# Compact score tables with one masked copy, and GpSimd's sums and products moved to VectorE

## The chip, the cores and the metric

The kernel runs on one core of a Trainium2 chip. A core has five engines that work side by side, each with its own instruction queue: TensorE (PE in the profile) does matrix products and transposes into PSUM; VectorE (DVE), ScalarE (ACT) and GpSimd (POOL) do elementwise work; SyncE (SP) issues most DMAs. PEld is TensorE's loading of weights, which overlaps its products. An engine takes its instructions in order, and an instruction waits until the data that it needs are there. The metric is the time of one execution on the device, in microseconds (us); lower is better.

## What is computed

One layer of an encoder: half a step of a SwiGLU feed-forward network (FFN), a mixer, another half FFN step and a last norm, over 1024 tokens of width 1024, in fp32. The mixer has two groups of heads that share one input projection: attention with four query and two key/value heads, and a gated recurrence with four heads that runs in both directions. In the reference, cut to what matters here:

```python
def hgrn2_chunk_scan(q, k, v, log_f):          # per head; f = exp(log_f), k = 1 - f
    ...
    scores = jnp.einsum('nhtd,nhtsd,nhsd->nhts', qc, decay, kc)
    intra = jnp.einsum('nhts,nhse->nhte', scores, vc)
    ...

def hgrn2_bidirectional(q, zf_fwd, zf_bwd, i, g, lb, out_gain):
    ...
    o_dir = hgrn2_chunk_scan(q_dir, k_dir, v_dir, g_dir)
    o = o_dir[:bsz] + flip(o_dir[bsz:])
    o = rms_norm(o, out_gain).reshape(bsz, seq_len, REC_WIDTH)
    return o * jax.nn.silu(g)

def gqa_bidirectional(q, k, v, q_gain, k_gain):
    q = apply_axial_rope(rms_norm(q, q_gain), tables) * (HEAD_DIM ** -0.5)
    k = apply_axial_rope(rms_norm(k, k_gain), tables)
    ...

def hybrid_mixer(x, ...):
    ...
    return jnp.concatenate([attn, rec.astype(attn.dtype)], axis=-1) @ w_out
```

`out_gain` is one weight for each of the 128 channels of a head, the same for all four heads.

## The kernel before

The stages follow one another: FFN 1, the mixer's input stage (`mixer_in`, with the recurrence in `hgrn`), attention with the output projection (`attention`), FFN 2. All products have fp32 operands split into a rounded high part and a rest (`split`, L89: a ScalarE copy, then a VectorE subtraction), with three products for one.

**The recurrence.** `hgrn(n, ...)` (L892) works on one head: 128 channels on the partitions, 1024 tokens in eight chunks of 128 along the columns. The scores within a chunk are built from the diagonal and seven levels with blocks of 1, 2, 4 ... 64 tokens. The diagonal's key is the sum `kd` of the keys of both directions (L915, GpSimd). At each level TensorE makes a table of local scores of key blocks with queries (`block_product`, L880: two products of 64 by 64 per chunk); the table is right only where the two tokens lie in sibling blocks, so VectorE copies it under a 0/1 mask (`copy_predicated`, L961) into the head's matrix `A`. For the levels below 64 only the two diagonal 64 by 64 quarters of a chunk are used, so each level takes two masked copies, of partitions 0 to 63 and 64 to 127. Level 64 fills the two other quarters, with two ScalarE copies (L958). Between the levels VectorE multiplies keys and queries by the decay of the sibling block (L948, L952), ScalarE copies what stays (L939), and VectorE multiplies pairs of decays (`tot`, L971 and L974). Then come transposes of the keys (`ktp`, L982), their ScalarE copies (L984), products with the values (`U`, L992), a scan over chunks on VectorE (L1000) and the output `o` (L1014).

**The norm.** `head_norm` (L1021) squares on ScalarE, sums on VectorE (L1030), takes the root on GpSimd (`rstd`, L86), multiplies on VectorE (L1033, L1038) and multiplies by the gain on GpSimd (L1043). It serves the recurrence's output (`on`), stored to DRAM by an SP DMA, and the rotary parts.

**Rotary parts.** `roped` (L1055) takes the query projection `aq` (1024 columns) and the key projection `ak` (512 columns) in four parts each: `head_norm`, a swap of halves by ScalarE copies (L1071), the cosine product on VectorE (L1076), the sine product on GpSimd (L1077), their sum on VectorE (L1078), an SP DMA.

**The order.** The heads of the recurrence run one after another with high priority; TensorE's other projections are fitted between: `ri` (values) and head 1's projections beside head 0, `aq` and head 2's beside head 1, head 3's beside head 2, `rgk` (recurrence gates and attention keys, which are roped) beside head 3, then `rgv`. Wide PSUM tiles of these projections (`pp`) and of the recurrence (`ph`) have two buffers each. The order on every queue is made when the program is built, by a scheduler that goes by its own estimates of durations, so it is made anew for changed code.

**Attention.** For each of eight row blocks `rec_out` (L1267) multiplies the stored recurrence output by its gate on GpSimd, transposes it into `rT`, splits that into `recT` (L1275) and projects it. `vectors` (L764) loads the small weights and the masks, in the middle of FFN 1.

Of the kernel before, what the change touches and what calls it, by code (L numbers as in the profile page):

```python
# [13 lines left out]
F32 = mybir.dt.float32  # L14
F32R = mybir.dt.float32r
I32 = mybir.dt.int32
U8 = mybir.dt.uint8
# [27 lines left out]
class Trunk:  # L45
    def __init__(self, ctx, tc, io):
# [6 lines left out]
        pool("base", bufs=1).tile([P, 248], F32, name="base")  # L53
# [710 lines left out]
    def vectors(self, tmp):  # L764
# [3 lines left out]
        rows = tmp.tile([n_lb + NQ, P], F32, name="rows", tag="raw")  # L768
        nc.sync.dma_start(rows[:n_lb, :], io["rec_lb_logits"].rearrange("s j (h p) -> (s j h) p", p=P))
        nc.sync.dma_start(rows[n_lb:, :], io["attn_out_norm"].rearrange("(h p) -> h p", p=P))  # L770
        pt = self.ps("rows_T", "u")
        n = n_lb + NQ
# [3 lines left out]
        self.attn_gain = cols[:, n_lb:n]  # L776
# [14 lines left out]
        self.masks = self.const.tile([P, len(LEVELS), P], U8, name="masks")  # L791
        mf = tmp.tile([P, len(LEVELS), P], F32, name="masks_f", tag="raw")
# [5 lines left out]
        for key in ("attn_q_norm", "attn_k_norm", "rec_out_norm"):  # L798
            g = self.const.tile([P, HD], F32, name=f"g_{key}")
            nc.sync.dma_start(g, io[key].partition_broadcast(P))  # L800
            self.small[key] = g
# [78 lines left out]
    def block_product(self, out, keys, queries, c, across):  # L880

        h = P // 2
        for g in range(2):
            to = 1 - g if across else g
            ks = slice(c * P + g * h, c * P + (g + 1) * h)
            qs = slice(c * P + to * h, c * P + (to + 1) * h)
            self.nc.tensor.matmul(
                out[g * h : (g + 1) * h, qs], keys[:, ks], queries[:, qs], start=True, stop=True,
                tile_position=(0, g * h),
            )  # L890

    def hgrn(self, n, q, f, v, pools, out):  # L892
# [22 lines left out]
        nc.gpsimd.tensor_add(kd, x[:, 0, 0, :], x[:, 1, 0, :])  # L915
        pd = self.ps(f"diag_{n}", "ph")
        for c in range(NCH):
            self.block_product(pd, kd, q, c, False)
        a = pools["A"].tile([P, T], F32, name=f"A_{n}", tag="A")
        av = a.rearrange("p (c t) -> p c t", t=P)  # L920
        pdv = pd.rearrange("p (c t) -> p c t", t=P)
        sides = (slice(0, P // 2), slice(P // 2, P))
        for r in sides:
            nc.scalar.copy(av[r, :, r], pdv[r, :, r])
        tot, cur = f, 0
        rest = x[:, 1]
        for lv, hw in enumerate(LEVELS):
            now, nxt = x[:, cur], x[:, 2 - cur]
            pl = self.ps(f"lv_{n}_{hw}", "ph")
            last = hw == LEVELS[-1]  # L930
            for c in range(NCH):
                self.block_product(pl, now[:, 0, :], now[:, 1, :], c, last)
# [22 lines left out]
            plv = pl.rearrange("p (c t) -> p c t", t=P)  # L955
            if last:
                for lo, hi in (sides, sides[::-1]):
# [664 lines left out]
```

## Time and profile before

| | before |
|---|---|
| median of 3 runs (lowest to highest) | 1950.05 us (1949.29 to 1950.25) |
| profiled execution | 1951.57 us |
| its span, first to last instruction | 1949.8 us |
| mean granted clock of TensorE | 0.996 |
| GpSimd busy | 769.0 us |
| instructions | 26362 |

How to read the lines of the profile that follow: a group of instructions is one line, "line engine operation out<-in shapes xcount | busy us, mean ns of one | idle time of the engine just before them, and what ended most of it". In a timeline a line begins with start and duration in us, and a bracket at its end gives the time for which the engine stood idle just before, and what ended that. In a table of stretches a line begins with the stretch and its length; the seventh column after the length (behind the five engines) is the granted clock of TensorE, as a share of full speed. L12 is line 12 of the program.

### The profile page before, as it was taken

The numbers are of one execution on the slowest core, as the hardware profiler recorded it, in microseconds if no ns is written. First come the engines' busy times: TensorE is split into PE (matmuls) and PEld (weight loads), VectorE is DVE, ScalarE is ACT, GpSimd is POOL, SyncE is SP. The second block draws the span as 40 slices with busy tenths as digits, with TensorE's granted clock in tenths as the row PEclk, the third lists the DMA queues.
The fourth block names the chain that finished last, engine by engine and source line by source line (L and its number), as shares of the span: only waits on it lengthen the run. The fifth ranks groups of instructions, "written<-read, shape, count | busy, mean of one in ns | idle before, by whom it ended". The sixth has DMA issues, their size and how long they took to land.

```text
span 1949.8 us, 26362 instructions
## 1 busy us (share of the span) xinstructions
PE 1913.0 (98%) x10025; PEld 1601.8 (82%) x10025; DVE 1275.4 (65%) x1582; ACT 800.8 (41%) x1280; POOL 769.0 (39%) x585
## 2 busy tenths in 40 slices
PE   9999999999999999999989999999999999999998
PEld 8888888887888788878868888888888888888886
DVE  8655665656876673878683556658556666657866
ACT  6333343324444433333333546645333333344344
POOL 2655554533660000241212324416644555436711
PEclk9999999999999999999989999999999999999999
DMA  8333333127775211122123542283433332258644
GB/s 263 112 120 103 111 112 108 61 97 287 256 224 170 101 43 55 33 82 82 32 74 122 160 170 76 76 271 108 141 103 103 99 113 86 84 190 306 216 122 163
DMA packets 213212, 255.12 MB, mean 131 GB/s; under 512 B 12742, under 2 KB 141018, under 8 KB 213084
## 3 DMA queue, kind: packets, MB, share of 16 engines
q1 hardware_dynamic: 204028, 223.01, 35.9%
q0 software_dynamic: 9056, 30.42, 4.0%
q8 instruction: 79, 1.29, 0.3%
q14 instruction: 49, 0.40, 0.1%
HBM read 183.12 MB, written 70.25 MB: 130 GB/s over the span
## 4 chain that ended last, share of the span: by engine, by line
PE 85%; DVE 8%; issue 2%; DMA 2%; ACT 1%; POOL 1%; DVEq 0%; POOLq 0%; SPq 0%; ACTq 0%
PE pa_ffn L298 17%; PE pd_ffn L298 11%; PE pya_ffn L684 7%; PE pc_ffn L298 6%; PE pb_ffn L298 6%; PE rec_ps L166 5%; PE pp_ffn L280 5%; PE pye_ffn L684 3%; PE pyd_ffn L684 3%; PE pyc_ffn L684 3%; PE ri_ps L829 2%; PE py L1245 2%; PE pa L1245 2%; PE rgv_ps L829 2%; PE pv L1217 2%
## 5 line engine op out<-in xcount | busy, mean ns | idle before, releaser
L94 DVE TENSOR_TENSOR hl_in_ffn_A<-raw_in_ffn,hl_in_ffn_A 128x512 fp32r<-128x512 f32 x120 | 177.7, 1481 | 93.7 <-ACT hl_in_ffn_A L93 93.5
L298 PE MATMUL pa_ffn<-ffn_T,hl_in_ffn_S 128*128 128x512 f32 x960 | 236.8, 389 | 0.0
L298 PE MATMUL pd_ffn<-ffn_B,hl_in_ffn_S 128*128 128x512 f32 x936 | 225.6, 389 | 0.0
L298 PEld LDWEIGHTS pa_ffn<-ffn_T,hl_in_ffn_S 128*128 128x128 f32 x960 | 180.2, 188 | 37.4
L298 PEld LDWEIGHTS pd_ffn<-ffn_B,hl_in_ffn_S 128*128 128x128 f32 x936 | 175.7, 188 | 36.5
L94 DVE TENSOR_TENSOR hl_in_ffn_S<-s_ffn,hl_in_ffn_S 128x512 fp32r<-128x512 f32 x160 | 141.1, 886 | 70.6 <-ACT hl_in_ffn_S L93 70.4
L93 ACT CAST hl_in_ffn_S<-s_ffn 128x512 fp32r<-128x512 f32 x160 | 99.0, 623 | 212.5 <-PE pd_ffn L298 159.3
L93 ACT CAST hl_in_ffn_A<-raw_in_ffn 128x512 fp32r<-128x512 f32 x120 | 74.9, 625 | 136.8 <-PE pc_ffn L298 70.6
L94 DVE TENSOR_TENSOR hl_out_ffn_S<-raw_out_ffn_S,hl_out_ffn_S 128x512 fp32r<-128x512 f32 (+1 forms) x88 | 106.4, 1221 | 37.7 <-ACT hl_out_ffn_S L93 37.7
L94 DVE TENSOR_TENSOR hl_out_ffn_A<-raw_out_ffn_A,hl_out_ffn_A 128x1024 fp32r<-128x1024 f32 (+1 forms) x66 | 94.7, 1448 | 53.6 <-ACT hl_out_ffn_A L93 53.2
L166 PE MATMUL rec_ps<-hm,hl_rec_w 128*128 128x512 f32 x528 | 125.2, 395 | 3.4 <-DVE aq L1038 2.6
L254 POOL TENSOR_TENSOR s_ffn<-s_ffn,raw_in_ffn 128x512 f32<-128x512 f32 x40 | 63.1, 1579 | 159.8 <-issue 104.9
L684 PE MATMUL pya_ffn<-hl_out_ffn_S 128*128 128x512 f32 x528 | 120.6, 389 | 0.3 <-DVE hl_out_ffn_S L94 0.3
L166 PEld LDWEIGHTS rec_ps<-hm,hl_rec_w 128*128 128x128 f32 x528 | 99.3, 190 | 25.0 <-ACT hl_rec_w L93 3.0
L298 PE MATMUL pa_ffn<-ffn_B,hl_in_ffn_A 128*128 128x512 f32 x480 | 116.9, 389 | 0.0
L684 PEld LDWEIGHTS pya_ffn<-hl_out_ffn_S 128*128 128x128 f32 x528 | 99.0, 188 | 21.2 <-DVE hl_out_ffn_S L94 0.7
L298 PE MATMUL pc_ffn<-ffn_T,hl_in_ffn_A 128*128 128x512 f32 x480 | 115.9, 389 | 0.0
L298 PE MATMUL pb_ffn<-ffn_B,hl_in_ffn_A 128*128 128x512 f32 x480 | 115.3, 389 | 0.0
L93 ACT CAST hl_out_ffn_S<-raw_out_ffn_S 128x512 fp32r<-128x512 f32 (+1 forms) x88 | 73.4, 837 | 94.0 <-PE pya_ffn L684 39.3
L253 POOL TENSOR_TENSOR s_ffn<-raw_in_ffn 128x512 f32<-128x512 f32 x40 | 52.1, 1301 | 135.6 <-DVE hl_in_ffn_S L94 135.4
L298 PEld LDWEIGHTS pb_ffn<-ffn_B,hl_in_ffn_A 128*128 128x128 f32 x480 | 90.1, 188 | 18.7
L298 PEld LDWEIGHTS pc_ffn<-ffn_T,hl_in_ffn_A 128*128 128x128 f32 x480 | 90.1, 188 | 18.7
(287 smaller groups left out, 3930.7 us busy)
## 6 DMA issues: line engine op xcount, KB each, us to landing
raw_in_ffn<-in_ffn_w_in SPq DMA_DIRECT2D x88, 512.0 KB, 4.2
raw_out_ffn_S<-d_comb SPq DMA_DIRECT2D x88, 256.0 KB, 2.7
d_comb<-g_ffn POOLq DMA_DIRECT2D x80, 256.0 KB, 2.3
raw_out_ffn_A<-d_act SPq DMA_DIRECT2D x66, 256.0 KB, 5.1
ffn_kept<-in_ffn_w_out SPq DMA_DIRECT2D x65, 256.0 KB, 5.4
d_act<-g_ffn SPq DMA_DIRECT2D x60, 256.0 KB, 2.3
raw_out_ffn_A<-in_ffn_w_out SPq DMA_DIRECT2D x52, 256.0 KB, 5.4
x<-d_x SPq DMA_DIRECT2D x24, 512.0 KB, 4.0
```

Of the source, the lines that this page charges most:

```text
L93: nc.scalar.copy(hl[:, 0, :], src)
L94: (lo_engine or nc.vector).tensor_sub(hl[:, 1, :], src, hl[:, 0, :].bitcast(F32))
L166: nc.tensor.matmul(out, hl[:, a, ks], h[half][b][:, k, cols], start=(k == 0 and i == 0), stop=(k == NK - 1 and i == 2),)
L253: nc.gpsimd.tensor_add(s1, a21, a22)
L254: nc.gpsimd.tensor_sub(s2, s1, a11)
L280: nc.tensor.matmul(halves(ps[j]), A[2 * j + k // 4][:, a, ks], B[k // 4][:, :, b, k % 4, lo:hi], start=(k == 0 and i == 0), stop=(k == NK ...
L298: nc.tensor.matmul(ps, A[:, a, ks], op(key)[:, b, k, :], start=(first and k == 0 and i == 0), stop=(k == 3 and i == 2), skip_group_check=True,
L684: nc.tensor.matmul(ps, hl[:, a, j * P : (j + 1) * P], hl[:, b, hi], start=(first and i == 0 and n == 0), stop=(i == last and n == 2), skip ...
L829: nc.tensor.matmul(ps[:, tt, :], h[half][a][:, k, ts], hl[j][:, b, ws], start=(k == 0 and i == 0), stop=(k == NK - 1 and i == 2),)
L1217: nc.tensor.matmul(ps, vt[:, j, a, vs], pT[j][:, b, i4, :], start=(st == 0 and i == 0), stop=(st == NT - 1 and i == 2),)
L1245: nc.tensor.matmul(py, lhs(a, n), units[n][:, b, ds], start=(n == 0 and i == 0), stop=(n == 3 and i == 2),)
```

## The change

Tables of local scores become compact: `half_tables` puts the two 64 by 64 quarters of a chunk into the same 64 columns, one on partitions 0 to 63 and one on 64 to 127, so that a level's table has 512 columns. One masked copy with all 128 partitions takes it into the first 64 columns of each chunk of `A`; the last level moves the second half to its place with three ScalarE copies. The masks shrink to six of 64 columns. `kd`, the gain product of `head_norm` and the sine product go from GpSimd to VectorE. The recurrence's norm weight is no longer applied in `head_norm` but at the split of `recT`, as a scale per partition, on ScalarE (high part) and VectorE (rest). The padding pool `base` takes up the freed 1024 bytes per partition.

```diff
-        pool("base", bufs=1).tile([P, 248], F32, name="base")
+        pool("base", bufs=1).tile([P, 504], F32, name="base")
...
         n_lb = 2 * 2 * NREC
-        rows = tmp.tile([n_lb + NQ, P], F32, name="rows", tag="raw")
+        n = n_lb + NQ + 1
+        rows = tmp.tile([n, P], F32, name="rows", tag="raw")
...
+        nc.sync.dma_start(rows[n - 1 :, :], io["rec_out_norm"].unsqueeze(0))
...
-        self.attn_gain = cols[:, n_lb:n]
+        self.attn_gain, self.rec_gain = cols[:, n_lb : n - 1], cols[:, n - 1 :]
...
-        self.masks = self.const.tile([P, len(LEVELS), P], U8, name="masks")
-        mf = tmp.tile([P, len(LEVELS), P], F32, name="masks_f", tag="raw")
+        shape = [P, len(LEVELS) - 1, P // 2]
+        self.masks = self.const.tile(shape, U8, name="masks")
+        mf = tmp.tile(shape, F32, name="masks_f", tag="raw")
...
-        for key in ("attn_q_norm", "attn_k_norm", "rec_out_norm"):
+        for key in ("attn_q_norm", "attn_k_norm"):
...
-    def block_product(self, out, keys, queries, c, across):
+    def half_tables(self, name, keys, queries, across=False):
 
         h = P // 2
-        for g in range(2):
-            to = 1 - g if across else g
-            ks = slice(c * P + g * h, c * P + (g + 1) * h)
-            qs = slice(c * P + to * h, c * P + (to + 1) * h)
-            self.nc.tensor.matmul(
-                out[g * h : (g + 1) * h, qs], keys[:, ks], queries[:, qs], start=True, stop=True,
-                tile_position=(0, g * h),
-            )
+        out = self.ps(name, "ph")[:, : T // 2].rearrange("p (c t) -> p c t", t=h)
+        for c in range(NCH):
+            for g in range(2):
+                to = 1 - g if across else g
+                ks = slice(c * P + g * h, c * P + (g + 1) * h)
+                qs = slice(c * P + to * h, c * P + (to + 1) * h)
+                self.nc.tensor.matmul(
+                    out[g * h : (g + 1) * h, c, :], keys[:, ks], queries[:, qs],
+                    start=True, stop=True, tile_position=(0, g * h),
+                )
+        return out
...
-        nc.gpsimd.tensor_add(kd, x[:, 0, 0, :], x[:, 1, 0, :])
-        pd = self.ps(f"diag_{n}", "ph")
-        for c in range(NCH):
-            self.block_product(pd, kd, q, c, False)
+        nc.vector.tensor_add(kd, x[:, 0, 0, :], x[:, 1, 0, :])
+        pd = self.half_tables(f"diag_{n}", kd, q)
...
-        sides = (slice(0, P // 2), slice(P // 2, P))
-        for r in sides:
-            nc.scalar.copy(av[r, :, r], pdv[r, :, r])
+        first, second = slice(0, P // 2), slice(P // 2, P)
+        same = av[:, :, first]
+        nc.scalar.copy(same, pd)
...
             if last:
-                for lo, hi in (sides, sides[::-1]):
-                    nc.scalar.copy(av[lo, :, hi], plv[lo, :, hi])
+                nc.scalar.copy(av[second, :, second], same[second])
+                nc.scalar.copy(av[first, :, second], pl[first])
+                nc.scalar.copy(same[second], pl[second])
             else:
-                for r in sides:
-                    nc.vector.copy_predicated(
-                        av[r, :, r],
-                        self.masks[r, lv : lv + 1, r].broadcast_to([P // 2, NCH, P // 2]),
-                        plv[r, :, r],
-                    )
+                nc.vector.copy_predicated(
+                    same, self.masks[:, lv : lv + 1, :].broadcast_to([P, NCH, P // 2]), pl
+                )
...
-        self.head_norm(o, po, NCH, self.small["rec_out_norm"], f"rec{n}")
+        self.head_norm(o, po, NCH, None, f"rec{n}")
...
-        nc.gpsimd.tensor_mul(ov, ov, gain.unsqueeze(1).broadcast_to([P, n, HD]))
+        if gain is not None:
+            nc.vector.tensor_mul(ov, ov, gain.unsqueeze(1).broadcast_to([P, n, HD]))
...
-            nc.gpsimd.tensor_mul(s4, s4, sin)
+            nc.vector.tensor_mul(s4, s4, sin)
...
-            self.split(rT, pt)
+            nc.scalar.mul(rT[:, 0, :], pt, self.rec_gain)
+            nc.vector.scalar_tensor_tensor(
+                out=rT[:, 1, :], in0=pt, scalar=self.rec_gain, in1=rT[:, 0, :].bitcast(F32),
+                op0=ALU.mult, op1=ALU.subtract,
+            )
```

## What is predicted, and from what

> **What bounds the kernel now.** I read the page first: its busy line, and the TensorE row of its forty slices.
>
> ```profile
> PE 1913.0 (98%) x10025; PEld 1601.8 (82%) x10025; DVE 1275.4 (65%) x1582; ACT 800.8 (41%) x1280; POOL 769.0 (39%) x585
> ...
> PE   9999999999999999999989999999999999999998
> ```
>
> TensorE (PE) is busy for 1913.0 us of a span of 1949.8. The change adds and removes no matrix product, so all that it can win is idle time of TensorE and time in which TensorE's clock is lowered: 36.8 us of idle in the whole span. VectorE (DVE) is busy 65%, but that is a mean over stages. The change works in the recurrence and rotary stage and, with one small edit, in attention. So the next view is the busy time of the engines in stretches of time; its columns are start:end, length, then busy us and instructions of PE, weight loads, DVE, ACT and POOL, and the granted clock.
>
> ```profile
> 690.00:1050.00 360.00, 345.62 (x2543) 290.57 (x2542) 252.38 (x346) 119.89 (x147) 75.52 (x36) 0.98 0.21 65
> 790.00:880.00 90.00, 85.51 (x626) 70.71 (x625) 73.22 (x91) 29.01 (x35) 30.42 (x14) 0.98 0.18 56
> 957.00:1010.00 53.00, 43.40 (x408) 36.21 (x407) 43.09 (x66) 20.32 (x28) 15.63 (x9) 0.90 0.13 41
> 1050.00:1300.00 250.00, 242.69 (x1410) 209.33 (x1409) 144.84 (x222) 134.21 (x238) 81.36 (x73) 1.00 0.38 128
> 875.00:880.00 5.00, 4.95 (x15) 3.94 (x16) 4.72 (x3) 2.27 (x4) 5.00 (x3) 0.66 0.00 0
> 1000.00:1005.00 5.00, 1.27 (x6) 1.30 (x7) 4.91 (x8) 2.10 (x3) 0.00 (x0) 0.50 0.18 52
> 1005.00:1010.00 5.00, 5.00 (x30) 4.87 (x29) 1.43 (x5) 3.02 (x4) 0.00 (x0) 0.67 0.31 108
> ```
>
> In 690 to 1050 TensorE idles 14.4 us; 4.5 of it falls in 790 to 880 (head 1, beside the rotary work on `aq`) and 9.6 in 957 to 1010 (head 3, beside that on `ak`). In both VectorE is busy 81% of the time. Attention (1050 to 1300) idles another 7.3, in pieces, where the change hardly works. The timeline of TensorE has five stops in the two stretches; the bracket gives the wait and what ended it.
>
> ```profile
> 834.23 1.06 PE L982 MATMUL ktp<-ident,hx 128*128 128x128 f32 x8 [1.92 <-DVE hx L952]
> ...
> 875.05 1.54 PE L166 MATMUL rec_ps<-hm,hl_rec_w 128*128 128x512 f32 x3 [2.58 <-DVE aq L1038]
> ...
> 978.94 1.15 PE L887 MATMUL lv<-hx 128*64 128x64 f32 x32 [2.80 <-DVE hx L952]
> ...
> 997.96 1.96 PE L887 MATMUL lv<-hx 128*64 128x64 f32 x32 [3.00 <-DVE hx L952]
> 1003.73 1.51 PE L982 MATMUL ktp<-ident,hx 128*128 128x128 f32 x6 [3.80 <-DVE tot L974]
> ```
>
> All five end with VectorE: 1.92 + 2.58 = 4.5 us and 2.80 + 3.00 + 3.80 = 9.6 us. Behind the second and the last the clock is granted at 0.66 (five us, (1 - 0.66) x 5 = 1.7 us lost) and at 0.50 and 0.67 (0.5 x 1.27 + 0.33 x 5 = 2.3 us). So the stage holds 14.1 + 1.7 + 2.3 = 18.1 us that a faster VectorE could give back.
>
> **The change part by part.** First the durations on VectorE, by line and shape (busy us, then mean ns), and of the GpSimd (POOL) work that goes.
>
> ```profile
> L961 DVE COPY_PREDICATED A<-masks,lv 64x512 f32<-64x512 uint8 x48 | 35.4, 738 | 1.3
> L948 DVE TENSOR_TENSOR hx<-hx,rf 128x256 f32<-128x256 f32 x16 | 17.4, 1110 | 0.0
> L1076 DVE TENSOR_TENSOR aq<-aq,rope_aq 128x1024 f32<-128x1024 f32 x4 | 11.6, 2894 | 5.0 <-ACT aq L1071 3.8 <-issue 1.2
> L971 DVE TENSOR_TENSOR tot<-rf 128x1024 f32<-128x1024 f32 x4 | 4.9, 1224 | 0.1
> L1078 DVE TENSOR_TENSOR ak<-ak,ak 128x512 f32<-128x512 f32 x4 | 2.7, 685 | 1.2 <-POOL ak L1077 1.2
> ```
> ```profile
> L915 POOL TENSOR_TENSOR kd<-hx 128x1024 f32<-128x1024 f32 x4 | 13.8, 3451 | 102.5 <-ACT hx L908 99.6 <-issue 2.8
> L1043 POOL TENSOR_TENSOR on<-on,g_rec_out_norm 128x1024 f32<-128x1024 f32 x4 | 10.0, 2508 | 3.2 <-DVE on L1033 2.8 <-issue 0.4
> L1043 POOL TENSOR_TENSOR aq<-aq,g_attn_q_norm 128x1024 f32<-128x1024 f32 x4 | 9.5, 2387 | 6.7 <-DVE aq L1038 6.7
> L1043 POOL TENSOR_TENSOR ak<-ak,g_attn_k_norm 128x512 f32<-128x512 f32 x4 | 5.1, 1273 | 5.7 <-issue 5.7
> ```
>
> *Masked copies.* 48 on 64 partitions become 24 on 128. The trace has none on 128 partitions. Bounds: 0.69 us (a two-input 128x512 product, L1078) and 1.48 (two of the old ones, so nothing won). ScalarE (ACT) decides for the low end: it copies 64x512 and 128x512 out of PSUM in the same time,
>
> ```profile
> L93 ACT CAST recT<-rT 128x512 fp32r<-128x512 f32 x8 | 4.8, 601 | 12.0 <-PE rT L1273 12.0
> L924 ACT COPY A<-diag 64x512 f32<-64x512 f32 x8 | 4.6, 581 | 10.6 <-PE diag L887 10.5
> L958 ACT COPY A<-lv 64x512 f32<-64x512 f32 x8 | 4.6, 576 | 0.0
> ```
>
> so columns count and not partitions, and I take 0.74: VectorE loses 24 x 0.74 = 17.8 us in all, 4.4 a head.
>
> *Sums and products that move to VectorE.* `kd`: 4 x 1.22 = 4.9 us. The gain and the sine product of `aq`: 8 x 1.22 = 9.8; of `ak`: 8 x 0.69 = 5.5. Together 20.2 us, more than the masked copies give back. But GpSimd's work is not free now, as the timeline shows:
>
> ```profile
> 692.68 3.06 POOL L915 TENSOR_TENSOR kd<-hx 128x1024 f32<-128x1024 f32 x1 [26.87 <-ACT hx L908]
> 693.41 2.81 DVE L948 TENSOR_TENSOR hx<-hx,rf 128x256 f32<-128x256 f32 x1
> ...
> 705.39 0.62 DVE L948 TENSOR_TENSOR hx<-hx,rf 128x256 f32<-128x256 f32 x1
> ...
> 821.59 1.28 DVE L952 TENSOR_TENSOR hx<-hx,tot 128x512 f32<-128x512 f32 x2
> ...
> 825.59 2.21 DVE L952 TENSOR_TENSOR hx<-hx,tot 128x512 f32<-128x512 f32 x2
> ...
> 827.72 0.19 DVE L974 TENSOR_TENSOR tot<-tot 128x48 f32<-128x48 f32 x1
> 827.84 3.47 DVE L952 TENSOR_TENSOR hx<-hx,tot 128x512 f32<-128x512 f32 x2
> ...
> 834.01 1.22 DVE L1076 TENSOR_TENSOR aq<-aq,rope_aq 128x1024 f32<-128x1024 f32 x1
> ...
> 846.89 3.46 DVE L1076 TENSOR_TENSOR aq<-aq,rope_aq 128x1024 f32<-128x1024 f32 x1 [1.23 <-issue]
> ...
> 974.26 1.82 DVE L1076 TENSOR_TENSOR ak<-ak,rope_ak 128x512 f32<-128x512 f32 x1 [4.00 <-ACT ak L1071]
> ...
> 997.73 1.27 DVE L974 TENSOR_TENSOR tot<-tot 128x48 f32<-128x48 f32 x1
> ```
>
> A VectorE product that begins under a GpSimd one ends about when that one ends: 2.81 for 0.62 under `kd` (692.68 + 3.06 = 695.74; it ends at 696.22), 3.46 for 1.22 beside the sine product, 1.27 for 0.19. Cosine and sine side by side take 3.46; one behind the other on VectorE they take 2.44.
>
> *Stops 1 and 2 (head 1).* VectorE loses, before 875: two level steps that were held up, (2.21 - 1.28) + (3.47 - 1.28) = 3.1; two of the three long cosine products (11.6 - 4 x 1.22 = 6.7 in three, so 2.2 each), 4.5; masked copies 4.4. It gains two products for each of three rotary parts, 6 x 1.22 = 7.3. Net -4.7; of it -3.1 - 4.4 + 2.4 = -5.1 lies ahead of stop 1, which needs 1.92. Stop 2 waits for the product of the fourth part, which frees a PSUM bank (L1038). Each part ahead of it gets shorter in its own chain: the gain 2.39 - 1.22 = 1.2, cosine and sine 3.46 - 2.44 = 1.0. Three parts make 6.6 for 2.58. I take both stops, 4.5, and the clock behind the second, 1.7.
>
> *Stops 3 to 5 (head 3).* VectorE stands still for 4.0 us at 970 to 974, behind a cosine product that waits for ScalarE's swap, which waits for GpSimd: `ak`'s gain (1.27) queued there behind the recurrence's gain (2.4). That one goes to attention, and `ak`'s becomes 0.69 on VectorE, then the swap, so 0.9 of waiting is left: -3.1. Masked copies -4.4; held-up steps: 1.82 - 0.69 = 1.1, 1.27 - 0.19 = 1.1, and about 1.0 under `kd`. Added: `kd` 1.2 and two parts' products, 4 x 0.69 = 2.8. Net -3.1 - 4.4 - 3.2 + 4.0 = -6.7 of the 9.6 that TensorE waits there; 2.9 stays. The lowered clock behind the last stop I leave in, since a stop of 2.58 was enough for one at 875.
>
> [...]
>
> *What costs nothing.* Heads 0 and 2 are quicker on VectorE too, but TensorE does not wait there (14.4 - 14.1 = 0.3 us), since projections lie between. The diagonal's copy becomes one instead of two, and the last level's three instead of two: ScalarE stays level. That last group gains a wait: it now stands behind the sixth masked copy, and behind it on ScalarE queue the copies of the transposed keys (L984), for which TensorE's U products wait. Three copies of 0.58 are 1.7 us; VectorE's two last products (2 x 1.22 = 2.4) run meanwhile and end later, and TensorE needs them first. Without that cover it is up to 1.7 us a head. In attention the copy gets a scale per partition: 0.60 from the row above, at most the 0.73 of the softmax's scaled one, 8 x 0.13 = 1.0 us on ScalarE; TensorE's waits there name no `recT`. The normalised output is stored 2.4 us earlier; no wait of TensorE names it. Masks, the extra row load and the dropped broadcast load lie under the first FFN, where TensorE does not stop; the padded pool keeps the later tiles in place.
>
> ```profile
> L1196 ACT ACTIVATE p<-p,rd 128x512 f32<-128x512 f32 x32 | 23.3, 731 | 5.5 <-DVE rd L1194 5.4
> ```
>
> *Sum.* 4.5 + 1.7 + 6.7 = 12.9 us. The profiled execution took 1951.57 us (span 1949.8 and 1.8 around it), 1.5 above the median of the runs, 1950.05. I take the 12.9 from the median: **1937.2**.
>
> **The rivals.** *All of it goes* (0.14). If the new order of work puts enough products beside head 3, 18.1 us come back: 1931.9. For it: VectorE loses some 3 us more in every other head; against it: head 3's chain stays VectorE's.
>
> *The masked copy costs double* (0.14), so it does not do what it says: nothing is won on 128 partitions. Stop 1 then gains 3.1 - 2.4 = 0.7, stop 2 still goes with its clock (4.3), head 3 gains 6.7 - 4.4 = 2.3: 7.3 in all, 1942.8. ScalarE's rows speak against it.
>
> *The stops move* (0.16). The order on TensorE is planned anew. If products of TensorE are drawn ahead by as much as VectorE gains, the next wait is for the two wide PSUM tiles, whose emptying still runs through a reduction and GpSimd's root, and under 3.9 us remain: 1946 to 1950.
>
> *VectorE becomes the bound* (0.10), on the other side. Place: head 1's rotary parts. If the long durations are not GpSimd's doing and stay, VectorE has 7.3 more and 4.4 less ahead of stop 2, and `kd` 1.2: 4.1 us later, with 1.7 for a longer low clock: 1955.9. It decides where the held-up products do not fall below about half of their excess. [...]
>
> **How the numbers follow.** The forecast's own band, 9 to 16 us back (1934 to 1941), gets 0.46. I call 0.2% (3.9 us) about what a measurement of this kernel can tell from no change. Faster: 0.46 + 0.14 + 0.14 = 0.74, and 0.01 of the moved stops; same 0.15; slower 0.10. The range from 1931 to 1948 takes in all of it coming back, the doubled copy and the better half of the moved stops, and leaves out the rest and the slower case.
>
> **What would show it.** Masked copies x24 near 740 ns (1480: the copy was mis-sized). L948 near 0.6 us and the cosine product near 1.22 throughout (if not, the hold-up was not GpSimd's). TensorE's idle in the recurrence stage near 3 us, with the stop at head 3's transposes left, and the clock full where the second stop was. It is wrong if TensorE's list of waits names ScalarE's copies of `A` or the swap in place of VectorE, or if attention's 7.3 us of idle changes by over 2.

## The result and the profile after

The changed kernel takes **1928.64 us** (median of 5 runs, 1927.95 to 1929.75); before took 1950.05 beside it (5 runs, 1949.29 to 1952.26). The ratio is 0.9889 (95% interval 0.9875 to 0.9904): 21.4 us come back, not 12.9, and the time lies 2.4 us below the lower end of the range.

The busy line of the page of after, and TensorE's row in forty slices:

```profile
PE 1905.8 (99%) x10025; PEld 1597.7 (83%) x10025; DVE 1250.9 (65%) x1578; ACT 802.1 (42%) x1280; POOL 714.1 (37%) x561
...
PE   9999999999999999999999999999999999999998
```

The slice at 8 in the middle is gone, and TensorE is *busy* for 7.2 us less although it does the same products. To see where, I cut both traces at the same events: first product of the recurrence's projections (`rec_ps`), last of `rgv_ps`, last of `pp_ffn` in attention. First the stretches of before, then those of after (start:end, length, busy us and instructions of PE, weight loads, DVE, ACT and POOL, granted clock, DMA share, GB/s):

```profile
0.00:678.00 678.00, 671.61 (x3086) 557.50 (x3086) 452.06 (x534) 284.30 (x471) 305.61 (x243) 1.00 0.47 153
678.00:1075.50 397.50, 382.67 (x2707) 321.05 (x2708) 264.49 (x362) 135.85 (x169) 78.64 (x38) 0.98 0.21 64
1075.50:1351.50 276.00, 268.10 (x1630) 234.51 (x1629) 172.94 (x262) 150.82 (x275) 101.35 (x88) 1.00 0.44 145
1351.50:1949.80 598.30, 590.62 (x2606) 488.74 (x2604) 385.93 (x427) 229.79 (x366) 283.36 (x217) 1.00 0.44 144
```

```profile
0.00:677.80 677.80, 671.62 (x3086) 557.67 (x3086) 450.00 (x534) 284.28 (x471) 307.50 (x243) 1.00 0.47 152
677.80:1054.10 376.30, 375.28 (x2708) 316.90 (x2709) 236.66 (x358) 136.55 (x169) 23.39 (x14) 1.00 0.22 68
1054.10:1329.30 275.20, 268.02 (x1630) 234.35 (x1629) 173.40 (x262) 151.44 (x275) 101.48 (x88) 1.00 0.44 146
1329.30:1927.60 598.30, 590.89 (x2606) 488.74 (x2604) 390.89 (x427) 229.83 (x366) 281.73 (x217) 1.00 0.44 144
```

All but 1.0 us of the 22.2 between the spans falls in the second row, the recurrence and rotary stage: 397.5 to 376.3, so 21.2. It has three parts:

- **Idle time of TensorE**: 397.50 - 382.67 = 14.8 us before, 376.30 - 375.28 = 1.0 after: 13.8 less.
- **Lowered clock**: summed over stretches of 1 us, (1 - granted clock) times TensorE's busy time is 4.9 us before and nothing after.
- **The rest of its busy time**: 382.67 - 4.9 = 377.8 before and 375.3 after: 2.5 less, for the same products.

VectorE is busy 27.8 us less in this stage (264.49 to 236.66), although the balance of its work, added up from durations, is +2.6: 20.2 us taken over, 17.6 of masked copies saved. The groups of its instructions after, by line and shape (busy us, mean ns, idle before):

```profile
L960 DVE COPY_PREDICATED A<-masks,lv 128x512 f32<-128x512 uint8 x24 | 17.8, 741 | 0.1
...
L948 DVE TENSOR_TENSOR hx<-hx,rf 128x256 f32<-128x256 f32 x16 | 9.8, 639 | 0.0
...
L920 DVE TENSOR_TENSOR kd<-hx 128x1024 f32<-128x1024 f32 x4 | 4.9, 1226 | 0.0
...
L1074 DVE TENSOR_TENSOR aq<-aq,rope_aq 128x1024 f32<-128x1024 f32 x4 | 4.9, 1222 | 0.7 <-ACT aq L1069 0.5
```

A masked copy of 128 partitions takes 741 ns, one of 64 took 738. The products that GpSimd had held up are short: L948 639 ns (1110 before), the cosine product of `aq` 1222 (2894). What TensorE still waits for in the stage is this list (us in total, times, longest):

```profile
PE ktp L979 <- DVE tot L971: 0.6, 1, 0.6
PE rec_ps L166 <- DVE hm L145: 0.4, 1, 0.4
```

Of the five stops one is left, at head 3's transposes, with 0.6 us in place of 3.80. The timeline of TensorE in head 3, from the last gate products ahead of its diagonal to its transposes, shows how. Before (the rows of the three stops are in the prediction):

```profile
956.90 9.57 PE L829 MATMUL rgk_ps<-hl_rgk_w,hm 128*128 128x512 f32 x41
966.39 1.15 PE L887 MATMUL diag<-rq,kd 128*64 128x64 f32 x32
967.48 4.15 PE L829 MATMUL rgk_ps<-hl_rgk_w,hm 128*128 128x512 f32 x17
971.56 2.09 PE L887 MATMUL lv<-hx 128*64 128x64 f32 x64
973.58 2.56 PE L829 MATMUL rgk_ps<-hl_rgk_w,hm 128*128 128x512 f32 x10
...
980.08 6.66 PE L829 MATMUL rgk_ps<-hl_rgk_w,hm 128*128 128x512 f32 x28
986.67 1.15 PE L887 MATMUL lv<-hx 128*64 128x64 f32 x32
987.75 1.88 PE L829 MATMUL rgk_ps<-hl_rgk_w,hm 128*128 128x512 f32 x7
...
990.64 3.24 PE L829 MATMUL rgk_ps<-hl_rgk_w,hm 128*128 128x512 f32 x13
```

After:

```profile
944.79 9.57 PE L831 MATMUL rgk_ps<-hl_rgk_w,hm 128*128 128x512 f32 x41
954.29 1.15 PE L891 MATMUL diag<-rq,kd 128*64 128x64 f32 x32
955.37 4.83 PE L831 MATMUL rgk_ps<-hl_rgk_w,hm 128*128 128x512 f32 x20
960.14 2.09 PE L891 MATMUL lv<-hx 128*64 128x64 f32 x64
962.15 5.28 PE L831 MATMUL rgk_ps<-hl_rgk_w,hm 128*128 128x512 f32 x22
967.37 2.08 PE L891 MATMUL lv<-hx 128*64 128x64 f32 x64
969.38 5.51 PE L831 MATMUL rgk_ps<-hl_rgk_w,hm 128*128 128x512 f32 x23
974.82 2.08 PE L891 MATMUL lv<-hx 128*64 128x64 f32 x64
976.83 5.28 PE L831 MATMUL rgk_ps<-hl_rgk_w,hm 128*128 128x512 f32 x22
982.04 1.15 PE L891 MATMUL lv<-hx 128*64 128x64 f32 x32
983.77 1.06 PE L979 MATMUL ktp<-ident,hx 128*128 128x128 f32 x8 [0.57 <-DVE tot L971]
```

Two things differ. Beside head 3's levels stand 20 + 22 + 23 + 22 = 87 gate products (`rgk_ps`; such products of another projection, on which TensorE works while a head's next table is not ready, I call the head's cover) where there were 17 + 10 + 28 + 7 + 13 = 75. And the level tables run mostly two at a time (64 products in one piece), so TensorE changes between tables and gate products less often.

### The profile page after: what moved, and what is told of

It reads as the page before. It is cut to its first block, busy times and chain, and to the rows that moved or that the text cites. A ratio compares the mean times of both kernels' runs of the same rounds, so it can differ in the third digit from the quotient of the medians.

```text
span 1927.6 us, 26292 instructions
## 1 busy us (share of the span) xinstructions
PE 1905.8 (99%) x10025; PEld 1597.7 (83%) x10025; DVE 1250.9 (65%) x1578; ACT 802.1 (42%) x1280; POOL 714.1 (37%) x561
## 4 chain that ended last, share of the span: by engine, by line
PE 90%; DVE 4%; DMA 3%; issue 1%; ACT 1%; POOL 0%; SPq 0%; DVEq 0%; POOLq 0%; ACTq 0%
PE pa_ffn L298 17%; PE pd_ffn L298 11%; PE pya_ffn L684 7%; PE rec_ps L166 6%; PE pc_ffn L298 6%; PE pb_ffn L298 6%; PE pp_ffn L280 5%; PE pye_ffn L684 3%; PE pyd_ffn L684 3%; PE pyc_ffn L684 3%; PE aq_ps L831 2%; PE ri_ps L831 2%; PE pa L1243 2%; PE rgv_ps L831 2%; PE pv L1215 2%; PE s L1183 2%
## 5 line engine op out<-in xcount | busy, mean ns | idle before, releaser
L94 DVE TENSOR_TENSOR hl_out_ffn_A<-raw_out_ffn_A,hl_out_ffn_A 128x1024 fp32r<-128x1024 f32 (+1 forms) x66 | 101.6, 1551 | 48.1 <-ACT hl_out_ffn_A L93 47.3
L94 DVE TENSOR_TENSOR hl_out_ffn_S<-raw_out_ffn_S,hl_out_ffn_S 128x512 fp32r<-128x512 f32 (+1 forms) x88 | 101.6, 1162 | 40.7 <-ACT hl_out_ffn_S L93 40.7
L684 PEld LDWEIGHTS pya_ffn<-hl_out_ffn_S 128*128 128x128 f32 x528 | 99.0, 188 | 21.4 <-DVE hl_out_ffn_S L94 1.0
L93 ACT CAST hl_out_ffn_S<-raw_out_ffn_S 128x512 fp32r<-128x512 f32 (+1 forms) x88 | 73.4, 837 | 95.7 <-PE pya_ffn L684 38.6
L298 PEld LDWEIGHTS pa_ffn<-ffn_B,hl_in_ffn_A 128*128 128x128 f32 x480 | 90.0, 188 | 18.7
```

Source lines behind the costliest of these rows:

```text
L93: nc.scalar.copy(hl[:, 0, :], src)
L94: (lo_engine or nc.vector).tensor_sub(hl[:, 1, :], src, hl[:, 0, :].bitcast(F32))
L298: nc.tensor.matmul(ps, A[:, a, ks], op(key)[:, b, k, :], start=(first and k == 0 and i == 0), stop=(k == 3 and i == 2), skip_group_check=True,
L684: nc.tensor.matmul(ps, hl[:, a, j * P : (j + 1) * P], hl[:, b, hi], start=(first and i == 0 and n == 0), stop=(i == last and n == 2), skip ...
```

## The experiments

The open question was where the 8.5 us beyond the forecast come from. In the runs by head below, theory A is the prediction's own reckoning: a stop is paid for by what VectorE saves in the head in which TensorE stops, and relief elsewhere is worth nothing. Theory B: VectorE's relief counts in every head, since products that are not used up as cover beside one head are left as cover for the next. The planner is the scheduler that orders the queues. For the other runs the text on record says what each letter expects.

All kernels compute the whole of the reference. The table puts the runs together: the median; the ratio to before, measured beside it, with its 95% interval; the length of the recurrence and rotary stage, cut as above; TensorE's idle time in it; what the lowered clock lost; the rest of its busy time; and in how many separate pieces the tables (the diagonal's among them), key transposes and `U` products stand in TensorE's order of instructions. A cost of 2 us is within the interval of a ratio; where I use one, the stage and its stops carry it. "Old" in a head means that the two masked copies and `kd` on GpSimd are back there.

| kernel | us | ratio | stage | idle | clock | rest | pieces |
|---|---|---|---|---|---|---|---|
| before | 1950.05 | 1 | 397.5 | 14.8 | 4.9 | 377.8 | 33 |
| after | 1928.64 | 0.9889 (0.9875 to 0.9904) | 376.3 | 1.0 | 0 | 375.3 | 28 |
| compact tables alone | 1940.33 | 0.9953 (0.9938 to 0.9968) | 385.4 | 7.7 | 1.7 | 376.0 | 30 |
| two copies a level again | 1943.07 | 0.9964 (0.9951 to 0.9977) | 390.9 | 10.1 | 2.9 | 377.9 | 33 |
| `kd` on GpSimd | 1930.83 | 0.9907 (0.9890 to 0.9923) | 377.5 | 1.7 | 0 | 375.8 | 29 |
| gain and sine on GpSimd | 1937.14 | 0.9938 (0.9924 to 0.9953) | 384.3 | 6.8 | 1.7 | 375.8 | 30 |
| sine on GpSimd | 1928.87 | 0.9888 (0.9871 to 0.9904) | 376.5 | 1.2 | 0 | 375.3 | 28 |
| gain on GpSimd | 1929.88 | 0.9894 (0.9879 to 0.9909) | 377.8 | 2.3 | 0 | 375.5 | 30 |
| recurrence weight on GpSimd | 1931.57 | 0.9897 (0.9880 to 0.9915) | 378.1 | 2.5 | 0 | 375.7 | 28 |
| heads 0 and 2 old | 1932.93 | 0.9903 (0.9885 to 0.9921) | 380.7 | 3.8 | 0 | 376.9 | 30 |
| heads 1 and 3 old | 1936.19 | 0.9920 (0.9904 to 0.9936) | 385.4 | 4.9 | 3.1 | 377.4 | 32 |
| head 0 old | 1930.81 | 0.9900 (0.9886 to 0.9915) | 378.1 | 2.2 | 0 | 375.9 | 29 |
| head 2 old | 1930.75 | 0.9899 (0.9885 to 0.9914) | 378.7 | 2.6 | 0 | 376.1 | 29 |
| head 3 old | 1933.84 | 0.9913 (0.9897 to 0.9930) | 382.2 | 3.8 | 1.7 | 376.7 | 30 |

**Compact tables alone.** Everything else as before; shown against the changed kernel:

```diff
-        nc.vector.tensor_add(kd, x[:, 0, 0, :], x[:, 1, 0, :])
+        nc.gpsimd.tensor_add(kd, x[:, 0, 0, :], x[:, 1, 0, :])
...
-        self.head_norm(o, po, NCH, None, f"rec{n}")
+        self.head_norm(o, po, NCH, self.small["rec_out_norm"], f"rec{n}")
...
-            nc.vector.tensor_mul(ov, ov, gain.unsqueeze(1).broadcast_to([P, n, HD]))
+            nc.gpsimd.tensor_mul(ov, ov, gain.unsqueeze(1).broadcast_to([P, n, HD]))
...
-            nc.vector.tensor_mul(s4, s4, sin)
+            nc.gpsimd.tensor_mul(s4, s4, sin)
```

> The kernel before with the compact tables and one masked copy alone; GpSimd keeps its sums and products. VectorE loses 24 x 0.74 = 17.8 us. Theory A (a part is worth its VectorE time in heads 1 and 3 alone, where TensorE stops): stop 1 goes (1.9), stop 2 stays since it hangs on the rotary chain with GpSimd in it, head 3 gains 4.4 of its 9.6: 6.3 us, 1943.7. Theory B (relief in any head is carried on, because head 3 then starts earlier against the products that fill its levels): head 3's stops go almost whole, 1.9 + 8 and the clock behind the last, 3: some 13 us, 1937. Rival C (all of the gain is GpSimd's hold on VectorE's reads): under 3 us, 1948; L948 and the cosine products stay near 1.1 and 2.9 us in all theories.

1940.33: the tables alone give 9.7 us, halfway between the two theories' times. The long durations are all there (L947 1108 ns, cosine of `aq` 3140), and three stops are left, of which only the last clearly belongs to the old list. TensorE's timeline in this run:

```profile
846.95 0.49 PE L1010 MATMUL o<-v_rec,A 128*128 128x128 f32 x2 [1.56 <-DVE hx L996]
863.64 16.66 PE L166 MATMUL rec_ps<-hm,hl_rec_w 128*128 128x512 f32 x72 [2.80 <-DVE hl_rec_w L94]
974.30 1.69 PE L890 MATMUL lv<-hx 128*64 128x64 f32 x32 [2.78 <-DVE hx L951]
```

Two stops have moved within head 1: behind the scan, and to the split of the next weights, which VectorE does late.

**Two copies a level.** The changed kernel with two masked copies of 64 partitions from the compact tables:

```diff
-                nc.vector.copy_predicated(
-                    same, self.masks[:, lv : lv + 1, :].broadcast_to([P, NCH, P // 2]), pl
-                )
+                for r in (first, second):
+                    nc.vector.copy_predicated(
+                        same[r], self.masks[r, lv : lv + 1, :].broadcast_to([P // 2, NCH, P // 2]), pl[r]
+                    )
```

> The changed kernel with each masked copy as two of 64 partitions out of the compact table; GpSimd's sums and products stay on VectorE. VectorE gets 17.8 us back. Theory A: 4.4 us more in head 3 alone, whose last stop returns with its clock, and head 1 stays free: 1928.6 + 4.4 + 2 = 1935. Theory B: head 3 also starts later against its fill by the time that heads 0 and 2 lose (4.4 us): 1938 or more. Rival C: 1930 or less.

1943.07, on B's side. This is the prediction's rival "the masked copy costs double", which was worked out at 7.3 us back (1942.8); 6.9 came back against the before measured beside it (1949.99). So the moves alone were priced about right in sum, in part by luck: heads 0 and 2 lose 2.2 us to stops that the working did not have, and head 3 gets 3.3 us of stops back (9.6 to 1.32 + 0.84 + 4.13) where it had 2.3. What was priced too low: the copies on top are worth 14.4 us, where the forecast had 12.9 - 7.3 = 5.6. The stage shows what they buy: 9.1 us of idle, 2.9 of clock, 2.6 of the rest. The copies take 738 ns each again, 48 of them, and the last stop in this run's timeline of TensorE is longer than before's 3.80:

```profile
996.32 3.65 PE L980 MATMUL ktp<-ident,hx 128*128 128x128 f32 x16 [4.13 <-DVE tot L972]
```

Here TensorE also stops in heads 0 and 2 (0.64 + 0.44 and 0.64 + 0.47 us), where before had none over 0.2.

**`kd` on GpSimd.**

```diff
-        nc.vector.tensor_add(kd, x[:, 0, 0, :], x[:, 1, 0, :])
+        nc.gpsimd.tensor_add(kd, x[:, 0, 0, :], x[:, 1, 0, :])
```

> The changed kernel with the sum kd back on GpSimd, nothing else. L948 under kd goes back to 2.8 us in each head (2.2 more), VectorE's own 1.22 go: 1.0 us net a head on VectorE, and the diagonal waits some 2 us longer in head 3. Theories A and B: 1929 to 1931. Rival C (the hold is the whole gain): a quarter to a third of 21 us, 1934 to 1936.

1930.83, as expected by both. The hold-up returns with it, and nothing else does:

```profile
L948 DVE TENSOR_TENSOR hx<-hx,rf 128x256 f32<-128x256 f32 x16 | 17.4, 1110 | 0.0
```

So 1110 against 639 ns is `kd`'s doing. By what means the one product holds up the other, no run shows; the "reads" of rival C were the author's assumption. One stop of 1.06 us comes in head 3.

**Gain and sine on GpSimd.**

```diff
-            nc.vector.tensor_mul(ov, ov, gain.unsqueeze(1).broadcast_to([P, n, HD]))
+            nc.gpsimd.tensor_mul(ov, ov, gain.unsqueeze(1).broadcast_to([P, n, HD]))
...
-            nc.vector.tensor_mul(s4, s4, sin)
+            nc.gpsimd.tensor_mul(s4, s4, sin)
```

> The changed kernel with the gain and the sine product of the rotary parts back on GpSimd; kd and the tables stay as changed and the recurrence's weight stays at the split. Cosine products go back to 2.9 us for aq, the level steps under them are held again. Theory A: stop 2 returns with its clock (4.3 us) and half of head 3's wait for the swap (2): 1935. Theory B: the masked copies have left enough slack, stop 2 returns at most in part: 1930 to 1933. Rival C: over 1938.

1937.14: 8.5 us over the changed kernel, more than A or B had, less than C. Stops of 1.60 and 2.82 stand in head 1 where the run of the tables alone has 1.56 and 2.80, and one of 1.92 at head 3's transposes. The cosine product of `aq` takes 3458 ns in the mean, all four held; in before three of four were, so the mean there was 2894.

**The sine alone, the gain alone** (the lower and the upper half of that diff).

> The changed kernel with the sine product alone back on GpSimd. Cosine and sine then run side by side and the cosine product is held to 3.4 us for aq and about 1.0 for ak: VectorE gains 2.4 - 3.4 = 1.0 us more a part than one behind the other. If the hold is what the rotary parts cost: 1931 to 1934. If what costs is GpSimd's place in the chain ahead of the swap (the gain): 1929 to 1930.

> The changed kernel with the gain alone back on GpSimd. The chain of a rotary part gets 1.2 us longer for aq and 0.6 for ak, and level steps that fall under the gain are held. If the chain is what costs: 1932 to 1936, with the stop at the projection behind aq back. If the hold on the cosine product is: 1929 to 1931.

1928.87 and 1929.88: 0.2 and 1.2 us, together 1.4, while both in one kernel cost 8.5. The sine run came out just under both of its ranges, the gain run in the second of its two. The timelines show a difference that goes with it. First the run with both on GpSimd:

```profile
841.46 2.39 POOL L1075 TENSOR_TENSOR aq<-aq,rope_aq 128x1024 f32<-128x1024 f32 x1 [1.25 <-ACT aq L1069]
841.47 3.46 DVE L1074 TENSOR_TENSOR aq<-aq,rope_aq 128x1024 f32<-128x1024 f32 x1 [2.46 <-ACT aq L1069]
```

Then the run with the sine alone on GpSimd:

```profile
839.63 1.23 DVE L1074 TENSOR_TENSOR aq<-aq,rope_aq 128x1024 f32<-128x1024 f32 x1 [1.05 <-ACT aq L1069]
839.68 3.45 POOL L1075 TENSOR_TENSOR aq<-aq,rope_aq 128x1024 f32<-128x1024 f32 x1 [3.81 <-ACT aq L1069]
```

Both wake at ScalarE's swap. Where GpSimd starts 10 ns ahead, its product takes 2.39 us and VectorE's ends 1.08 behind it, 3.46 long. Where VectorE starts 50 ns ahead, its product takes 1.23 and GpSimd's 3.45. All four cosine products of `aq` are long in the first run (3.44 to 3.47) and short in the second (1.22 or 1.23), and the second kernel's time can't be told from that of after. That the order of start makes up the difference is argued and not shown by itself: with both on GpSimd its gain also lengthens the chain ahead of the swap. Another pair of the run with the sine alone speaks against the order by itself: there GpSimd's product starts at 825.58, 1.26 us ahead, and takes 4.73, and VectorE's, from 826.84, still takes 1.22.

**The recurrence's weight back in its norm, on GpSimd.**

```diff
-        self.head_norm(o, po, NCH, None, f"rec{n}")
+        self.head_norm(o, po, NCH, self.small["rec_out_norm"], f"rec{n}")
...
-            nc.vector.tensor_mul(ov, ov, gain.unsqueeze(1).broadcast_to([P, n, HD]))
+            (nc.gpsimd if flat else nc.vector).tensor_mul(ov, ov, gain.unsqueeze(1).broadcast_to([P, n, HD]))
...
-            nc.scalar.mul(rT[:, 0, :], pt, self.rec_gain)
...
+            self.split(rT, pt)
```

> The changed kernel with the recurrence's weight back in its norm, on GpSimd, and the plain split in attention. VectorE waits again at head 3's first rotary part for GpSimd, which takes 2.4 us for that product, unless the gain of ak, now on VectorE, no longer queues behind it. Theory A and B: ak's gain is on VectorE, so at most 1 us: 1928 to 1930. Rival (the queue on GpSimd was the cause of the 4.0 us stand): 1931 to 1932.

1931.57, in the rival's range and not in that of A or B, but not by the rival's mechanism: the cosine products of `ak` wait for the swap no longer than after (1.6 us in four, both times). What is longer is VectorE's work under GpSimd's gain. In head 3 it is the gain product of `ak`, 2.54 us where after has 0.69:

```profile
957.20 2.40 POOL L1041 TENSOR_TENSOR on<-on,g_rec_out_norm 128x1024 f32<-128x1024 f32 x1 [0.52 <-DVE on L1030]
957.60 2.54 DVE L1041 TENSOR_TENSOR ak<-ak,g_attn_k_norm 128x512 f32<-128x512 f32 x1
```

Behind it TensorE stops in head 3 for 0.86 and 0.50 us, at tables, and for 0.63 at the transposes, there behind ScalarE's copies of `A`. One sine product of `aq` in head 1 is held in the same way (3.43 us), and no stop follows it there.

**By head.** Heads 0 and 2 old:

```diff
-        nc.vector.tensor_add(kd, x[:, 0, 0, :], x[:, 1, 0, :])
+        (nc.vector if n in (1, 3) else nc.gpsimd).tensor_add(kd, x[:, 0, 0, :], x[:, 1, 0, :])
...
-                nc.vector.copy_predicated(
-                    same, self.masks[:, lv : lv + 1, :].broadcast_to([P, NCH, P // 2]), pl
-                )
+                for r in (slice(0, P),) if n in (1, 3) else (first, second):
+                    nc.vector.copy_predicated(
+                        same[r], self.masks[r, lv : lv + 1, :].broadcast_to([r.stop - r.start, NCH, P // 2]), pl[r]
+                    )
```

> The changed kernel with one masked copy and kd on VectorE only in heads 1 and 3; heads 0 and 2 take two masked copies of 64 partitions and kd on GpSimd, as before. TensorE does not stop in heads 0 and 2 in either kernel. Theory A (relief there is worth nothing, as the prediction had it): 1928.6 to 1929.5. Theory B (it is carried into head 3, which starts 15 fill products earlier): head 3 has to find its fill after a start 2 x 0.235 x 7 = 3 us later, so 2 to 6 us more, 1931 to 1935.

1932.93: 4.3 us, as B expected; A (1928.6 to 1929.5) falls. The stops are in the old heads themselves (0.67 + 0.43 in head 0, 0.64 + 0.47 in head 2) and, with 1.11 in place of 0.57, in head 3, which was not touched.

Heads 1 and 3 old, with the same edit in both places:

```diff
+                for r in (slice(0, P),) if n in (0, 2) else (first, second):
```

> The mirror: one masked copy and kd on VectorE only in heads 0 and 2, two copies and kd on GpSimd in heads 1 and 3. Theory A: heads 1 and 3 lose 4.4 + 1.0 each; head 1 has slack, head 3's last stop returns with its clock: 1928.6 + 5.4 + 2 = 1936. Theory B: part of it is saved by heads 0 and 2: 1931 to 1934, so about what the mirror run gives.

1936.19, where A had it, in part by luck; B missed. A expected slack in head 1 and the stop at head 3's transposes. TensorE stops for 0.63 and 0.50 us in head 1, and in head 3 at the gate products. The rows of this run, TensorE's and then ScalarE's:

```profile
974.67 7.70 PE L831 MATMUL rgk_ps<-hl_rgk_w,hm 128*128 128x512 f32 x20 [2.83 <-ACT rg L1085]
```

```profile
971.66 1.04 ACT L939 COPY hx<-hx 128x1024 f32<-128x1024 f32 x1 [3.03 <-DVE hx L952]
972.73 1.28 ACT L1085 ACT_TABLE_LOAD   x1
974.02 0.60 ACT L1085 ACTIVATE rg<-rgk_ps 128x512 f32<-128x512 f32 x1
```

The gate (`rg`) empties a bank that the next gate products need. ScalarE has it behind a level copy, and that copy waits 3.03 us for VectorE; a table load of 1.28 us stands between the two. So the slow VectorE stops TensorE by way of ScalarE's queue.

Head 0, head 2 and head 3 old, each alone (`n != 0`, `n != 2`, `n != 3` in the same two places):

> The changed kernel, but head 0 alone takes two masked copies of 64 partitions and kd on GpSimd. Theory B in its narrow form: only head 2 hands its relief on, because only head 3's projection (rgk) starts to run within the head before; head 1 always starts after 24 products of its fill. So nothing is lost here: 1928.6 to 1930. Wide form (relief of any head is carried on): half of what was lost with heads 0 and 2 both old, 1930.5 to 1931.

> The same with head 2 alone old. Narrow form: all of the 4.3 us that heads 0 and 2 together cost, 1932 to 1934, with TensorE's stops in head 3 and not in head 2. Wide form: half of it, 1930.5 to 1931. The prediction's own step (relief where TensorE does not wait is worth nothing): 1929.

> The changed kernel, but head 3 alone takes two masked copies of 64 partitions and kd on GpSimd: 4.4 + 1.0 us more for VectorE in that head. Heads 0 and 2 alone cost 2.2 and 2.1 us, the two heads 1 and 3 together 7.6. If every head is worth the same: 1930.8. If head 3 has used up its fill (141 of the 144 rgk products that two wide PSUM tiles and the one being emptied allow ahead of its transposes), the added time shows there as a stop of 3 us or more, with the lowered clock behind it: 1934 to 1936, and TensorE waits for ScalarE's gate or VectorE in 970 to 995.

1930.81, 1930.75 and 1933.84: 2.2, 2.1 and 5.2 us. For heads 0 and 2 the narrow form (head 0 worth at most 1.4 us; all of it through head 2, at 1932 to 1934) missed in both runs, and the wide one held: each has its price, and 2.2 + 2.1 is what both cost together. Heads 1 and 3 together cost 7.6, so some 2.4 is left for head 1, if the two add up. Head 0 stops in itself (0.62 + 0.45). Head 2 does so too (0.64 + 0.44), and one more stop follows in head 3, in the run with head 2 old:

```profile
986.50 4.62 PE L831 MATMUL rgk_ps<-hl_rgk_w,hm 128*128 128x512 f32 x19 [1.09 <-ACT rg L1085]
```

The run with heads 0 and 2 old has the same stop with 1.11. Head 3 alone came out a little under the 1934 to 1936 expected, by the mechanism expected: the stop at the gate of 2.83 us, and 1.7 lost to the clock.

## Why the prediction was wrong, step by step

Right were the bound, the place and the mechanism. TensorE was the bound, the stage was the recurrence and rotary one, all five stops hung on VectorE, and VectorE got shorter by less copying and because GpSimd no longer holds it. Masked copies x24 near 740 ns: 741. L948 near 0.6 and the cosine near 1.22: 0.64 and 1.22. The stop at head 3's transposes is the one left, and after's list of waits names neither ScalarE's copies of `A` nor the swap. Attention's idle time went from 7.9 to 7.2 us, so its edits cost nothing that shows.

Stops 1 and 2: 4.5 us forecast, and both are gone. What failed are three terms, 8.0 of the 8.5 us.

- **"2.9 stays", at head 3: 2.3 us too little.** 9.6 us of stops became 0.6, so 9.0 went and not 6.7. From diagonal to transposes it took 1003.73 - 966.39 = 37.3 us before and 983.77 - 954.29 = 29.5 after: VectorE's chain is 7.9 shorter, not 6.7 (its own rows, from the head's first product to the end of the `tot` that TensorE waits for, give 46.5 and 38.6). Most of that 1.2 is in the masked copies: the sum took durations, but along a chain what counts is the time from one start to the next. So counted, head 3's twelve old copies take 9.0 us and the six new ones 3.8, which is 5.3 less and not 4.4: two in a row take 1.50 to 1.55, one of 128 partitions 0.61 to 0.64. First two rows of before, then two of after:

```profile
980.63 1.52 DVE L961 COPY_PREDICATED A<-masks,lv 64x512 f32<-64x512 uint8 x2
982.18 1.29 DVE L952 TENSOR_TENSOR hx<-hx,tot 128x512 f32<-128x512 f32 x2
```

```profile
965.46 0.73 DVE L960 COPY_PREDICATED A<-masks,lv 128x512 f32<-128x512 uint8 x1
966.09 1.27 DVE L952 TENSOR_TENSOR hx<-hx,tot 128x512 f32<-128x512 f32 x2
```

The other 1.2 us of the 2.3 is more TensorE work within that chain: 37.3 - 9.6 = 27.7 before, 29.5 - 0.6 = 28.9 after. Twelve more gate products stand there, 2.7 us by the 0.225 from start to start (20 in 4.77, 22 in 5.22), against the half clock and the changes between tables and gate products that went. They were there to be had because head 3 begins after 54 gate products and not after 69, by TensorE's order. That is where "Heads 0 and 2 are quicker on VectorE too, but TensorE does not wait there" went wrong. It doesn't wait there because the planner gives these heads enough cover; a quicker head takes less of it (81 products of the next projections between head 2's diagonal and its transposes, and not 98), and what it doesn't take is left for the next. The runs by head give heads 0 and 2 a price of 4.3 us, where the step had none. Of it 2.2 us are stops in these two heads themselves, and only 0.5 shows as a longer stop in head 3; so the price is shown, and that it is handed on from head to head only in part.
- **"The lowered clock behind the last stop I leave in": 3.2 us too little.** The loss was 4.9 us and not the 4.0 that I counted, since the clock was down from 998 on, behind the stop of 3.00, and my rows began at 1000. All of it went, not 1.7, for no stop longer than 0.6 is left. This hangs on the first term: with 2.9 us of stop, the clock might have stayed down (below).
- **"All that it can win is idle time of TensorE and time in which TensorE's clock is lowered": 2.5 us too little.** TensorE's busy time at full clock is not fixed. Over the kernels it goes with the number of separate pieces: 377.8 and 377.9 us at 33, 377.4 at 32, 375.5 to 376.9 at 30, 375.3 to 375.7 at 28, so about 0.5 us for a piece more. (The pieces of level tables alone put the kernels in better order: 377.4 to 377.9 at 19, 376.7 and 376.9 at 18, 375.9 and 376.1 at 17, 375.3 to 376.0 at 16.) The timelines of head 3 give nearly as much: 32 table products take 1.08 us from start to start (986.67 to 987.75) and 64 take 2.01, 0.15 less than twice that, and a piece of gate products pays 4.77 - 20 x 0.225 = 0.27 beside its products. A VectorE that is ahead lets the planner put two tables into one piece. Some 0.6 of the 2.5, by my estimate, is no matter of pieces: the product ahead of a stop counts as busy for its whole length (a gate product's row is 396 ns in the mean before, 395 after), where the next one otherwise starts after some 0.23 us, and after has fewer stops. No run changes the pieces alone, so their share is argued from these figures.

Of the rivals, "all of it goes" was the one that came, under its own condition ("if the new order of work puts enough products beside head 3"). Its 18.1 us lacked 0.9 of the clock and the 2.5 of the pieces. The doubled copy fell with 741 ns, though its 7.3 us came near the 6.9 of the run that has it. The moved stops fell with the list of waits, but were no fancy: the runs with heads 1 and 3 old and with head 3 old stop for a PSUM tile to be emptied, though by ScalarE's gate and not by the reduction and root that were named, and with the tables alone the stops move to the scan and the weights. VectorE as the bound fell with the short durations.

The parts don't add up; the likely reason is that each takes VectorE further from the point at which TensorE stops. Tables alone gave 9.7 us and the moves alone 6.9, both together 21.4. Taken away one at a time, the single copy costs 14.4, gain and sine 8.5, the recurrence's weight 2.9 and `kd` 2.2, which is 28.0. No kernel tried was quicker than the changed one; the sine on GpSimd makes no difference (1928.87).

**What stays open.** That head 3's last stop went because head 3 began earlier is argued from the two orders, not shown by itself. With head 2 old, head 3 begins after 61 gate products, as that reading wants, but the planner then puts 102 beside its levels, the stop at the transposes doesn't return, and one at the gate comes in its place. A run with the new durations in the old order would settle it; the order isn't written by hand, and that wasn't tried.

## What to carry to other kernels

Where a planner fits an engine's free work as cover around several chains, "the bound engine does not wait here" doesn't price a relief at nothing: ask how much cover the chain takes now, and who gets what it no longer takes. Count the changes between small and large products into the bound engine's busy time, and the clock behind a stop into the stop. And before work is moved off an engine to GpSimd, see what VectorE has under way beside it: here 20 us of work moved *to* VectorE, and its busy time in the stage fell, from 244.1 us with the compact tables alone to 236.7.

## What the runs showed of the hardware

- **The length of a stop did not by itself tell whether the clock fell; where the stop lay went with it too.** The granted clock went to 0.50 behind stops of 2.58 and 3.00 us (before), 2.78 (tables alone), 2.82 (gain and sine), 2.83 (heads 1 and 3 old, head 3 old) and 4.13 (two copies). It stayed full behind one of 2.80 in before (978.94) and one of 2.80 in the run of the tables alone (863.64), and behind every stop up to 1.92. The loss was 1.7 to 3.2 us where it came. The half clock lasted 3.41 us (the first fall of before, tables alone, gain and sine, head 3 old), 6.83 (two copies, heads 1 and 3 old) or 10.24 (the second fall of before), one, two or three times 3.41, and the two falls of before, at 875.13 and 998.01, are 122.9 us apart, 36 times that. Cut into stretches of 3.41 us from these points, before's stop of 2.58 lies whole in one stretch and its stop of 2.80 is split between two (TensorE's busy time is the second figure):

```profile
871.72:875.13 3.41, 0.83 (x5) 0.40 (x3) 1.57 (x4) 1.96 (x2) 3.12 (x2) 1.00 0.57 171
875.13:878.54 3.41, 3.41 (x9) 2.63 (x10) 3.26 (x3) 0.93 (x2) 3.41 (x3) 0.50 0.00 0
974.12:977.53 3.41, 2.02 (x9) 1.31 (x7) 3.21 (x4) 2.34 (x3) 1.30 (x1) 1.00 0.30 88
977.53:980.95 3.42, 2.01 (x36) 1.78 (x37) 3.39 (x6) 0.86 (x2) 0.00 (x0) 1.00 0.38 119
```

Over the six kernels whose clock fell in this stage, the stretch ahead of each of the seven falls held 2.06 to 3.12 us of idle time, and no stretch that left the clock full held more than 1.86. That the clock goes by such stretches is a reading of these seven falls; no run moves a stop and nothing else.
- **The same cosine product of VectorE took 3.46 us beside one sine product of GpSimd and 1.23 beside another**: 3.46 where GpSimd's started 10 ns ahead (gain and sine on GpSimd, 841.47) and 1.23 where its own start was 50 ns ahead (sine alone, 839.63). The order of start by itself does not decide it, since the one at 826.84 took 1.22 with GpSimd's 1.26 us ahead.
- **A masked copy took as long on 128 partitions as on 64**: 738 ns for 64x512 (before) and 741 for 128x512 (after).
